# A state-space chunk's decay with the larger of two sums instead of a minimum with zero, its exponential head by head, and one multiply of the norm on GpSimd

## The chip, the cores and the metric

The kernel runs on one core of one Trainium2 chip. Its time is the device time of one execution in microseconds (us); the figure given is the median of the runs. The engines are named as in the profile: PE is TensorE's matmul, PEld its weight load, DVE is VectorE, ACT is ScalarE, POOL is GpSimd, SP is SyncE, which here starts transfers.

## The reference, cut to what matters

One inference step of a two-layer trunk for a prompt of 512 rows and a sample of 64 rows, 1024 columns wide. A layer projects the normed rows, sends part of the columns through a state-space scan (32 heads of 64 in 4 groups, state 128), part through windowed attention, merges both and adds a feed-forward block. The change lies in the scan and in the norm behind it:

```python
def step(state, inp):                      # one chunk, all heads
    xdt, da, bc, cc = inp
    acum = jnp.cumsum(da, axis=1)          # da = dt * a, a < 0: the sums fall
    seg = acum[:, :, None, :] - acum[:, None, :, :]
    decay = jnp.exp(jnp.where(causal[None, :, :, None], seg, -jnp.inf))
    cb = jnp.einsum("blgn,bsgn->blsg", cc, bc)
    y_in = jnp.einsum("blsg,blsgh,bsghp->blghp", cb, decay, xg)
    y_past = jnp.einsum("blgn,bghpn->blghp", cc, sg) * jnp.exp(acum)...
    tail = jnp.exp(acum[:, -1:] - acum)...
    new = sg * jnp.exp(acum[:, -1])... + jnp.einsum("blgn,blgh,blghp->bghpn", bc, tail, xg)
    return new, y_in + y_past
...
y = (y + xh * d_skip[:, None]).reshape(b, L, D_INNER) * jax.nn.silu(z)
y = rmsnorm(y.reshape(b, L, SSM_GROUPS, D_INNER // SSM_GROUPS), ssm_norm_g)   # x / rms, times a weight
```

## The kernel before, in words

All 576 rows (512 of the prompt, 64 of the sample) go through the layer together; activations stand with the columns on the 128 partitions and the rows along the free side. A large product is computed three times over, so that it comes out near full precision: `dps += hh*whi`, `dps += hh*wlo`, `dps += hl*whi` (L278, L279, L280), one 128x288 matmul each. `whi` is the rounded weight tile, made on ACT (L166), and `wlo` what the rounding left, made from `raw` and `whi` by POOL or DVE (L167). Weight tiles of the kinds `whi` and `wlo` have four buffers each.

The state-space part of a group g is a generator, `ssd(g)`, whose steps are let in between the units of the large products of the same stretch: one step of it behind each unit. There are five chunks in each of the 4 groups of the 2 layers, so 40 chunks: 32 of 128 rows and 8 of 64. A chunk goes through

- `step_a`: PE turns the chunk's `xT` (`xn`, L860) and multiplies B and C (`cb`, L862); `bc` holds the cumulative sums of the group's 8 heads along the free side, on every partition (loaded from `ac_dr`, a copy in DRAM). `seg` is the decay of the chunk, 8 heads x 128 x 128: DVE subtracts the sums of the partition's own row (L156, `seg<-bc,ac`), takes the minimum with zero (L869, `seg<-seg`), and ACT does one exponential over all of it (L159, `seg<-seg`). ACT then raises `bc` itself, for the part that comes from the state before.
- `step_p`: DVE makes `xd`, `xw` (input times step and times tail), then `seg<-seg,cbm` and `bc<-bc,BC`.
- `step_s`: `bn`, `xwh`, `xwl`, the pieces of B and of `xw` for the new state.
- `step_b`: PE multiplies `yp` (16 small matmuls, L916 `yp<-seg,xd` and, from the second chunk on, L921 `yp<-bc,S`) and `sp` (L926); DVE adds `yp` into `xT` (L153) and updates the state `S`.

`norm_g(g)` divides the group's gated output by its root mean square: `gbc` holds 1/rms on every partition (ACT copies it out of PSUM, L1035 and L1038). For four blocks of 128x576, DVE multiplies by it (L156, `xT<-xT,gbc`), ACT scales and rounds into `yh` (L159) and DVE makes the rest `yl` (L153). `yh` and `yl` are the moving operands of the group's branch product, which comes later.

Each engine works through its instructions in the order of the program. A scheduler sets that order when the kernel is built, so one edit can move instructions that the edit doesn't touch, on every engine.

## Time and profile before

| | |
|---|---|
| median of 3 runs | 2574.25 us (2573.8 to 2574.63) |
| profiled execution: its own time | 2575.55 us |
| profiled execution: its span | 2573.8 us |
| busy share of the span: PE, DVE, ACT, POOL | 98%, 63%, 41%, 41% |
| instructions: PE, DVE, ACT, POOL | 19609, 2991, 2383, 968 |

The span is the time from the first to the last recorded instruction; the profiled execution took 1.75 us more than that, and 1.30 us more than the median of the runs. A time such as 1411.94 is counted from the start of the span. PE is busy nearly all the time, so the kernel can change its time only through the 2% in which PE stands idle, through the clock at which PE runs, or by taking PE's work late.

### The profile page before, as it was taken

What the parts mean: (1) busy time and instruction counts of PE and PEld (TensorE: products, weight loads), DVE (VectorE), ACT (ScalarE), POOL (GpSimd) and SP (SyncE); (2) the same over time, 40 slices, a digit from 0 to 9 for tenths busy, and PEclk for the clock granted to TensorE, in tenths of its full rate; (3) what the DMA queues carried; (4) which work ended last, traced back from release to release, by engine and by line L of the source; (5) the groups of instructions that cost most, each with busy time, mean ns of one, the idle gap of its engine ahead of it and who ended that gap; (6) DMA issues with size and microseconds to landing.
All of it is one profiled execution on the core that took longest, in us unless ns stands there. A gap on an engine that the chain in (4) does not pass through costs nothing.

```text
span 2573.8 us, 49262 instructions
## 1 busy us (share of the span) xinstructions
PE 2520.1 (98%) x19609; PEld 2395.0 (93%) x19609; DVE 1611.3 (63%) x2991; ACT 1060.8 (41%) x2383; POOL 1054.9 (41%) x968
## 2 busy tenths in 40 slices
PE   7999999999999999999999999999999999999999
PEld 6888999999889999999988899999988999999999
DVE  4598677745765765565686995956467656444443
ACT  3445454443453532222355454543444445323222
POOL 3444455343225754444586464553422266000000
PEclk8999999999999999999999999999999999999999
DMA  8555523243224555545574333332321255222222
GB/s 230 159 157 157 152 86 99 81 103 76 54 58 118 162 166 155 166 140 154 158 183 128 91 95 103 93 102 79 94 70 50 78 147 150 83 83 83 83 79 75
DMA packets 464107, 294.34 MB, mean 114 GB/s; under 512 B 69093, under 2 KB 446405, under 8 KB 463877
## 3 DMA queue, kind: packets, MB, share of 16 engines
q1 hardware_dynamic: 463876, 291.18, 39.4%
q8 instruction: 155, 2.54, 0.4%
q14 instruction: 76, 0.61, 0.1%
HBM read 276.98 MB, written 13.16 MB: 113 GB/s over the span
## 4 chain that ended last, share of the span: by engine, by line
PE 74%; DVE 14%; issue 3%; POOL 2%; ACT 1%; DMA 1%; ACTq 0%; SPq 0%; POOLq 0%; DVEq 0%
PE dps L278 22%; PE dps L280 22%; PE dps L279 21%; DVE cv L153 3%; DVE xT L153 2%; DVE seg L156 1%; PE sc L1213 1%; POOL wlo L167 1%; PE pv L1276 1%; PE pT L1260 1%; PE sp L926 1%; DVE hl L156 1%; PE yp L916 1%; DVE bc L156 1%; DVE S L156 1%
## 5 line engine op out<-in xcount | busy, mean ns | idle before, releaser
L167 POOL TENSOR_TENSOR wlo<-raw,whi 128x512 fp32r<-128x512 f32 (+1 forms) x632 | 896.8, 1427 | 857.6 <-ACT whi L166 743.7
L278 PE MATMUL dps<-hh,whi 128*128 128x288 f32 x3536 | 1055.8, 299 | 4.0 <-ACT hh L672 2.8
L279 PE MATMUL dps<-hh,wlo 128*128 128x288 f32 x3536 | 1050.0, 297 | 2.4 <-POOL wlo L167 2.4
L280 PE MATMUL dps<-hl,whi 128*128 128x288 f32 x3536 | 1049.7, 297 | 1.2 <-DVE hl L156 1.1
L166 ACT CAST whi<-raw 128x512 fp32r<-128x512 f32 (+1 forms) x762 | 462.0, 610 | 555.6 <-PE dps L280 433.2
L278 PEld LDWEIGHTS dps<-hh,whi 128*128 128x128 f32 x3536 | 665.1, 188 | 26.1 <-issue 16.4
L279 PEld LDWEIGHTS dps<-hh,wlo 128*128 128x128 f32 x3536 | 666.3, 188 | 11.3 <-issue 5.4
L280 PEld LDWEIGHTS dps<-hl,whi 128*128 128x128 f32 x3536 | 665.9, 188 | 8.1 <-issue 5.3
L279 PE MATMUL dps<-ah,wlo 128*128 128x288 f32 x704 | 210.8, 299 | 3.7 <-POOL wlo L167 3.7
L278 PE MATMUL dps<-ah,whi 128*128 128x288 f32 x704 | 207.8, 296 | 3.1 <-ACT ah L166 2.6
L280 PE MATMUL dps<-al,whi 128*128 128x288 f32 x704 | 208.3, 296 | 0.0
L153 DVE SCALAR_TENSOR_TENSOR ada_acc<-araw,csl,ada_acc 128x1024 f32<-128x1024 f32 x98 | 153.2, 1602 | 70.1 <-DMA araw<-in_ada_w_dram 66.2
L153 DVE SCALAR_TENSOR_TENSOR cv<-u,colB,cv 128x579 f32<-128x579 f32 x144 | 146.1, 1014 | 30.3 <-ACT cv L159 22.9
L278 PE MATMUL dps<-yh,whi 128*128 128x288 f32 x512 | 153.0, 299 | 1.2 <-ACT u L808 1.1
L280 PE MATMUL dps<-yl,whi 128*128 128x288 f32 x512 | 153.8, 300 | 0.0
L279 PE MATMUL dps<-yh,wlo 128*128 128x288 f32 x512 | 151.7, 296 | 0.0
L279 PEld LDWEIGHTS dps<-ah,wlo 128*128 128x128 f32 x704 | 132.8, 189 | 6.7 <-POOL wlo L167 5.5
L167 DVE TENSOR_TENSOR wlo<-raw,whi 128x512 fp32r<-128x512 f32 (+1 forms) x124 | 83.7, 675 | 87.2 <-ACT whi L166 85.8
L278 PEld LDWEIGHTS dps<-ah,whi 128*128 128x128 f32 x704 | 132.6, 189 | 4.0 <-ACT ah L166 2.8
L280 PEld LDWEIGHTS dps<-al,whi 128*128 128x128 f32 x704 | 132.8, 189 | 0.2 <-DVE al L167 0.2
L278 PEld LDWEIGHTS dps<-yh,whi 128*128 128x128 f32 x512 | 97.3, 190 | 4.5 <-issue 1.9
L280 PEld LDWEIGHTS dps<-yl,whi 128*128 128x128 f32 x512 | 97.3, 190 | 2.0 <-issue 1.8
(326 smaller groups left out, 3863.6 us busy)
## 6 DMA issues: line engine op xcount, KB each, us to landing
raw<-in_w_in_dram SPq DMA_DIRECT2D x119, 512.0 KB
raw<-in_w_gate_up_dram SPq DMA_DIRECT2D x100, 512.0 KB
araw<-in_ada_w_dram SPq DMA_DIRECT2D x56, 512.0 KB
bc<-ac_dr SPq DMA_DIRECT2D x32, 512.0 KB
raw<-in_w_br_ssm_dram SPq DMA_DIRECT2D x32, 512.0 KB
raw<-in_w_out_dram SPq DMA_DIRECT2D x32, 512.0 KB
raw<-in_w_down_dram SPq DMA_DIRECT2D x32, 512.0 KB
raw<-in_ada_w_dram SPq DMA_DIRECT2D x24, 512.0 KB
```

The source lines that it names most:

```text
L153: V.scalar_tensor_tensor(out=out, in0=in0, scalar=scalar, in1=in1, op0=op0, op1=op1)
L156: V.tensor_tensor(out=out, in0=in0, in1=in1, op=op)
L166: S.copy(out=hi, in_=src)
L167: (eng or V).tensor_tensor(out=lo, in0=src, in1=f32(hi), op=ALU.subtract)
L278: T.matmul(ps, lhsT=wh, rhs=rh, start=a == 0, stop=False)
L279: T.matmul(ps, lhsT=wl, rhs=rh, start=False, stop=False)
L280: T.matmul(ps, lhsT=wh, rhs=rl, start=False, stop=a == nk - 1)
L916: T.matmul(yp[64 * r:64 * r + 64, m * 128:m * 128 + Lc], lhsT=xd[0:Lc, h, :], rhs=seg[0:Lc, h, 0:Lc], start=m == 0, stop=sprev is None and ...
L926: T.matmul(sp, lhsT=bn[0:Lc, i], rhs=xw[j], start=a == 0, stop=a == 2)
L1213: T.matmul(ps[:, pi * 192:pi * 192 + nk], lhsT=q[64 * r:64 * r + 64, pi, ch].rearrange("p h q -> p (h q)"), rhs=kT[64 * r:64 * r + 64, t, ...
L1260: T.transpose(ps[0:n, pi * 128:(pi + 1) * 128], s[:, r, pi, 64 * pi * (half is not None):][:, 0:n], ident)
L1276: T.matmul(ps[64 * r:64 * r + 64, 0:256], lhsT=vn[0:n, vt, cols[r]], rhs=pts[r][0:n, 0:256], start=True, stop=half is None)
```

## The change

`ac`, the cumulative sums with the row on the partition, becomes `nac`, the same with the sign turned, and so does the copy in DRAM from which `bc` is loaded. The decay of a chunk was exp(min(bc - ac, 0)). Now DVE takes the larger of the negated sums, max(bc, nac), and ACT computes exp(-seg + nac) head by head: eight instructions of 128x128 with a bias for each partition in place of one of 128x1024. The minimum with zero on DVE is gone. In `norm_g` the multiply by `gbc` runs on POOL and not on DVE.

```diff
-            ac = sm("ac", [128, 5, 32], bufs=1)
-            V.tensor_copy(out=ac.rearrange("p c h -> p (c h)"), in_=ps[:, 0:160])
+            nac = sm("nac", [128, 5, 32], bufs=1)
+            V.tensor_scalar(out=nac.rearrange("p c h -> p (c h)"), in0=ps[:, 0:160], scalar1=-1.0, scalar2=None,
+                            op0=ALU.mult)
...
-            tt(tw.rearrange("p c h -> p (c h)"), ps[:, 160:320], ac.rearrange("p c h -> p (c h)"), ALU.subtract)
+            tt(tw.rearrange("p c h -> p (c h)"), ps[:, 160:320], nac.rearrange("p c h -> p (c h)"), ALU.add)
...
-            S.copy(out=aT[:, 0:512], in_=p1[0:32, :])
-            S.copy(out=aT[:, 512:576], in_=p2[0:32, 0:64])
+            S.mul(out=aT[:, 0:512], in_=p1[0:32, :], mul=-1.0)
+            S.mul(out=aT[:, 512:576], in_=p2[0:32, 0:64], mul=-1.0)
...
                 tt(sg, bc[0:Lc, :, 0:Lc],
-                   st["ac"][0:Lc, ch, h0:h0 + 8].unsqueeze(2).to_broadcast([Lc, 8, Lc]), ALU.subtract)
-                V.tensor_scalar(out=sg, in0=sg, scalar1=0.0, scalar2=None, op0=ALU.min)
-                act(seg[0:Lc, :, 0:Lc], seg[0:Lc, :, 0:Lc], ACTF.Exp)
+                   st["nac"][0:Lc, ch, h0:h0 + 8].unsqueeze(2).to_broadcast([Lc, 8, Lc]), ALU.max)
+                for h in range(8):
+                    act(seg[0:Lc, h, 0:Lc], seg[0:Lc, h, 0:Lc], ACTF.Exp, scale=-1.0,
+                        bias=st["nac"][0:Lc, ch, h0 + h:h0 + h + 1])
                 if ch != 0:
-                    act(bc[:, :, 0:Lc], bc[:, :, 0:Lc], ACTF.Exp)
+                    act(bc[:, :, 0:Lc], bc[:, :, 0:Lc], ACTF.Exp, scale=-1.0)
...
             for j in range(4):
-                tt(y[:, j], y[:, j], bcs, ALU.mult)
+                G.tensor_tensor(out=y[:, j], in0=y[:, j], in1=bcs, op=ALU.mult)
```

The scheduler answers by moving other instructions. On PE, at the head of group 0 of layer 1, the program before has the turn of the first chunks' `xT` (`xn`) and the large product (`dps`) in this order:

```order
L956 MATMUL si<-ident,sld 128x128 x4
L860 MATMUL xn<-ident,xT 64x128 x3
L862 MATMUL cb<-BC 64x64
L864 MATMUL cb<-ident,BC 64x128
L278 MATMUL dps<-hh,whi 128x288
...
L279 MATMUL dps<-hh,wlo 128x288
L860 MATMUL xn<-ident,xT 64x128
L280 MATMUL dps<-hl,whi 128x288
...
L280 MATMUL dps<-hl,whi 128x288
L860 MATMUL xn<-ident,xT 128x128 x4
L862 MATMUL cb<-BC 128x128
```

and the changed program has there:

```order
L959 MATMUL si<-ident,sld 128x128 x4
L861 MATMUL xn<-ident,xT 64x128 x2
L863 MATMUL cb<-BC 64x64
L861 MATMUL xn<-ident,xT 64x128
L865 MATMUL cb<-ident,BC 64x128
L278 MATMUL dps<-hh,whi 128x288
...
L280 MATMUL dps<-hl,whi 128x288
L861 MATMUL xn<-ident,xT 128x128 x3
L863 MATMUL cb<-BC 128x128
...
L278 MATMUL dps<-hh,whi 128x288
L861 MATMUL xn<-ident,xT 128x128
L279 MATMUL dps<-hh,wlo 128x288
L861 MATMUL xn<-ident,xT 64x128
```

The last 64x128 turn of `xT` stood behind 17 `dps` matmuls, counted from the `cb` rows; it now stands behind 35. The lines 860 to 865 are the same as 859 to 864 of before, moved by one.

On POOL, at the norm of the fourth group of layer 0 (`ss` sums squares, `g_y` is the power that makes 1/rms), the program before has:

```order
L1018 TENSOR_TENSOR ss<-ss,nt 128x288 x2
L167 TENSOR_TENSOR wlo<-raw,whi 128x512 x2
L1018 TENSOR_TENSOR ss<-ss,nt 128x288
L167 TENSOR_TENSOR wlo<-raw,whi 128x512
L149 TENSOR_TENSOR g_y<-gv,mhalf 128x5
L167 TENSOR_TENSOR wlo<-raw,whi 128x512 x81
L149 TENSOR_TENSOR n_y<-nv,mhalf 128x3
```

and the changed program:

```order
L1021 TENSOR_TENSOR ss<-ss,nt 128x288
L167 TENSOR_TENSOR wlo<-raw,whi 128x512
L149 TENSOR_TENSOR g_y<-gv,mhalf 128x5
L167 TENSOR_TENSOR wlo<-raw,whi 128x512
L1045 TENSOR_TENSOR xT<-xT,gbc 128x576 x4
L167 TENSOR_TENSOR wlo<-raw,whi 128x512 x80
L149 TENSOR_TENSOR n_y<-nv,mhalf 128x3
```

The four multiplies now stand in one piece between two tiles of `wlo`; 80 tiles follow them, where 81 in a row stood before.

On DVE, at the last chunk of group 3 of layer 0 (`acc` takes the results of the branch product), the program before has:

```order
L156 TENSOR_TENSOR xd<-xn,dtv 128x512
L156 TENSOR_TENSOR xw<-xn,tw 128x512
L156 TENSOR_TENSOR seg<-bc,ac 128x1024
L156 TENSOR_TENSOR cbm<-cb,triu 128x128
L156 TENSOR_TENSOR acc<-acc,dps 128x288 x2
L869 TENSOR_SCALAR seg<-seg 128x1024
L156 TENSOR_TENSOR acc<-acc,dps 128x288
L156 TENSOR_TENSOR bc<-bc,BC 128x1024
L156 TENSOR_TENSOR seg<-seg,cbm 128x1024
L153 SCALAR_TENSOR_TENSOR xT<-xT,dsk_292,yp 128x128 x4
L156 TENSOR_TENSOR S<-S,el 128x512
```

and the changed program:

```order
L156 TENSOR_TENSOR xd<-xn,dtv 128x512
L156 TENSOR_TENSOR xw<-xn,tw 128x512
L156 TENSOR_TENSOR seg<-bc,nac 128x1024
L156 TENSOR_TENSOR cbm<-cb,triu 128x128
L156 TENSOR_TENSOR acc<-acc,dps 128x288 x3
L156 TENSOR_TENSOR seg<-seg,cbm 128x1024
L153 SCALAR_TENSOR_TENSOR xT<-xT,dsk_292,yp 128x128 x4
L156 TENSOR_TENSOR S<-S,el 128x512
L156 TENSOR_TENSOR bc<-bc,BC 128x1024
```

L869 is gone, and `bc<-bc,BC` has moved from ahead of `seg<-seg,cbm` to behind the four additions to `xT` and the step of the state. On ACT, at the same chunk, the program before has:

```order
L166 CAST xwh<-xw 128x512
L166 CAST bn<-cb 128x128
L166 CAST whi<-raw 128x512 x2
L159 ACTIVATE bc<-bc 128x1024
L159 ACTIVATE seg<-seg 128x1024
L166 CAST xwh<-xw 128x512
L166 CAST bn<-cb 128x128
```

and the changed program:

```order
L166 CAST xwh<-xw 128x512
L166 CAST bn<-cb 128x128
L166 CAST whi<-raw 128x512 x2
L159 ACTIVATE seg<-seg,nac 128x128 x8
L159 ACTIVATE bc<-bc 128x1024
L166 CAST xwh<-xw 128x512
L166 CAST bn<-cb 128x128
```

The eight exponentials of `seg` now come ahead of that of `bc`.

## Rows read from the trace of the kernel before

**Rows 1.** The page, part 1: busy us by engine, share of the span, instructions.

```profile
PE 2520.1 (98%) x19609; PEld 2395.0 (93%) x19609; DVE 1611.3 (63%) x2991; ACT 1060.8 (41%) x2383; POOL 1054.9 (41%) x968
```

**Rows 2.** Busy time by engine in the two state-space stretches, granted clock, DMA.

```profile
110.00:520.00 410.00, 402.00 (x3321) 374.18 (x3320) 313.49 (x526) 191.84 (x380) 193.27 (x180) 1.00 0.43 127
1385.00:1800.00 415.00, 404.45 (x3281) 388.90 (x3280) 321.47 (x536) 200.85 (x397) 210.15 (x188) 0.99 0.33 95
```

**Rows 3.** PE's waits: 110 to 520 us (first two), 1385 to 1800 us (total, times, longest).

```profile
PE si L956 <- DMA sld<-in_state_ssm_dram: 2.4, 1, 2.4
PE sp L926 <- DVE xT L153: 1.9, 1, 1.9
...
PE sp L926 <- DVE xT L153: 3.9, 2, 2.0
PE xn L860 <- DVE xT L153: 2.4, 1, 2.4
```

**Rows 4.** Timeline of PE around 1412 us: start, duration, instruction, idle time before it.

```profile
1411.81 0.29 PE L278 MATMUL dps<-hh,whi 128*128 128x288 f32 x1
1411.94 0.29 PE L279 MATMUL dps<-hh,wlo 128*128 128x288 f32 x1
1414.67 0.30 PE L860 MATMUL xn<-ident,xT 128*64 128x128 f32 x1 [2.44 <-DVE xT L153]
1414.73 0.38 PE L280 MATMUL dps<-hl,whi 128*128 128x288 f32 x1
...
1415.45 0.45 PE L278 MATMUL dps<-hh,whi 128*128 128x288 f32 x1
1415.69 0.45 PE L279 MATMUL dps<-hh,wlo 128*128 128x288 f32 x1
```

**Rows 5.** Busy times and PE's granted clock, 1415 to 1418.5 us.

```profile
1415.00:1418.50 3.50, 3.50 (x18) 3.49 (x18) 3.50 (x5) 1.42 (x3) 0.91 (x1) 0.53 0.35 96
```

**Rows 6.** Groups by line and shape: busy us, mean ns; idle before and releaser.

```profile
L167 POOL TENSOR_TENSOR wlo<-raw,whi 128x512 fp32r<-128x512 f32 x600 | 856.2, 1435 | 851.7 <-ACT whi L166 738.2 <-issue 38.3 <-PE pT L1263 23.8
...
L159 ACT ACTIVATE seg<-seg 128x1024 f32<-128x1024 f32 x32 | 33.9, 1061 | 22.8 <-DVE seg L869 22.4
...
L156 DVE TENSOR_TENSOR xT<-xT,gbc 128x576 f32<-128x576 f32 x32 | 29.9, 994 | 11.5 <-ACT gbc L1038 11.5
...
L869 DVE TENSOR_SCALAR seg<-seg 128x1024 f32<-128x1024 f32 x32 | 25.9, 810 | 0.0
...
L159 ACT ACTIVATE s<-s,nm 128x128 f32<-128x128 f32 x16 | 6.2, 390 | 10.7 <-DVE nm L153 10.7
```

**Rows 7.** Timeline around the last chunk of group 3, layer 0.

```profile
498.53 1.05 ACT L159 ACTIVATE bc<-bc 128x1024 f32<-128x1024 f32 x1
...
499.77 1.06 ACT L159 ACTIVATE seg<-seg 128x1024 f32<-128x1024 f32 x1 [0.19 <-DVE seg L869]
...
501.89 1.21 DVE L156 TENSOR_TENSOR seg<-seg,cbm 128x1024 f32<-128x1024 f32 x1
...
504.71 1.09 PE L916 MATMUL yp<-seg,xd 128*64 128x128 f32 x16
```

**Rows 8.** Timeline around the norm of group 3, layer 0.

```profile
565.13 0.59 ACT L1035 COPY gbc<-gbp 128x512 f32<-128x512 f32 x1 [0.20 <-PE gbp L1034]
...
565.61 0.22 ACT L1038 COPY gbc<-gbp 128x64 f32<-128x64 f32 x1
...
567.04 1.40 POOL L167 TENSOR_TENSOR wlo<-raw,whi 128x512 fp32r<-128x512 f32 x1 [3.39 <-ACT whi L166]
...
574.19 0.29 PE L279 MATMUL dps<-hh,wlo 128*128 128x288 f32 x1
```

**Rows 9.** Timeline of POOL and DVE at the norm of group 0, layer 0.

```profile
245.07 5.39 POOL L167 TENSOR_TENSOR wlo<-raw,whi 128x512 fp32r<-128x512 f32 x1 [5.45 <-ACT gbc L1038]
...
246.56 2.76 DVE L156 TENSOR_TENSOR xT<-xT,gbc 128x576 f32<-128x576 f32 x4
...
251.26 1.29 POOL L167 TENSOR_TENSOR wlo<-raw,whi 128x512 fp32r<-128x512 f32 x1
```

More of the change, by code (lines that the diff above doesn't have):

```diff
@@ L790, in dt_side @@
             SY.dma_start(out=ac_dr[l][4, :, 0:64], in_=aT[:, 512:576])
-            st.update(dt=dt, ac=ac, el=el, tw=tw)
+            st.update(dt=dt, nac=nac, el=el, tw=tw)
             yield
```

## Prediction, made before the changed kernel ran

> **What bounds the kernel now.** I read the page first. Its line of busy times shows PE at 2520.1 of 2573.8 us, 98%, and DVE, ACT and POOL at 63%, 41% and 41% [rows 1]. So the time is PE's work plus what PE loses, and an edit on DVE, ACT or POOL counts only where PE waits for that engine. The view by windows says how much can be lost or won where the changed instructions stand: in the two state-space stretches PE is busy 402.00 of 410 us and 404.45 of 415 us, so it stands idle for 8.00 + 10.55 = 18.55 us [rows 2]. DVE is busy 313 and 321 us there, ACT 192 and 201, POOL 193 and 210; none of them is near full over the stretch, and what matters is single places.
>
> The view of PE's waits names these places. The longest single waits are one of 2.4 us for the loaded state (`si`), one of 2.4 for DVE's `xT` (`xn`), and three of about 1.9 each, 5.8 in total, of `sp` for DVE's additions to `xT` [rows 3]. The timeline shows one of them with what follows it. Up to 1411.94 the `dps` matmuls start every 0.13 us. Then PE stands for 2.44 us in front of the fourth 64x128 `xn`, and a little later the matmuls start every 0.24 us (1415.45, 1415.69) [rows 4]. The granted clock over 1415.0 to 1418.5 is 0.53 [rows 5]: the lower of the two levels, 1.2 in place of 2.4 GHz, for most of these 3.5 us. The gap thus costs twice: 2.44 us of standing, and about (1 - 0.53) x 3.5 = 1.65 us of slow running behind it.
>
> **The change part by part.**
>
> *The minimum is removed.* DVE loses 32 instructions of 810 ns, 25.9 us busy [rows 6], and 8 short ones, which at half the elements on half the partitions I take at no more than the same 0.81 each, so 6.5 at the most. The larger-of-two that replaces the subtraction has the same operands and shape, so I cost it at no difference. What DVE wins does not reach PE by itself; it has to be looked for at the waits below.
>
> *One exponential becomes eight, on ACT.* The one takes 1061 ns for 128x1024. The nearest row for a 128x128 piece with a bias for each partition is the attention's `s<-s,nm`, 390 ns [rows 6]. Neighbours on ACT overlap: the copy of `gbc` that starts at 565.13 lasts to 565.72, and the next starts at 565.61, 0.11 us earlier [rows 8]. So eight take 8 x (0.39 - 0.11) + 0.11 = 2.35 us, 1.29 more than one. Below, I bound it by no loss (eight as quick as one), above by no overlap at all: 3.12 us, 2.06 more. Over 40 chunks that is 52 us (0 to 82) on an engine that is 41% busy [rows 1]. Is it on the path? At the chunk that I found to be among the tightest, the last of its group, ACT did the exponential of `bc` at 498.53 and that of `seg` from 499.77 to 500.83, because it waited for the minimum on DVE. DVE multiplied by `cbm` from 501.89 to 503.10, and PE used the result at 504.71 [rows 7]: 1.61 us to spare. In the changed order the eight come first, with no minimum to wait for: from 498.53 to 500.88, against 500.83 before. By the upper bound they end at 501.65, which is still before 501.89, where DVE took `seg` up. So the extra work on ACT is hidden by the minimum that is gone and by the exchange with `bc`; the exponential of `bc` ends about 1.1 us later, and DVE's `bc<-bc,BC` stands after the additions to `xT` in the new order anyway. I take 0. If that cover were gone (eight at 3.12 behind a late start), the loss is 2.06 - 1.61 = 0.45 us in each of 8 groups, +3.6 us, my upper bound. Copies with a factor of -1 in place of plain copies (`nac`, `aT`) have the same shapes and stand once in a layer: 0.
>
> *The multiply by 1/rms moves to POOL.* DVE loses 32 of 994 ns, 29.9 us. On POOL the nearest row is `wlo`, two inputs too, 128x512 in 1435 ns; by elements 1435 x 576/512 = 1.61 us each, 52 us in eight bursts of four [rows 6]. The undisturbed one of 1.29 gives 1.45 [rows 9], the lower bound. Queued behind a burst are weight tiles that PE needs. In the fourth group of layer 0 `gbc` is ready at 565.83; POOL then starts `wlo` at 567.04, and it ends at 568.44; I followed that tile by its buffer number to the matmul that first reads it, at 574.19 [rows 8]. That is a reserve of 5.75 us. Now the burst goes first: 565.83 + 4 x 1.61 = 572.27, then 1.40, so 573.67, and 0.52 us are left. I take 0, but the cover is thin: from 574.19 - 1.40 - 565.83 = 6.96, a multiply above 1.74 us makes PE wait. `yh` and `yl` come later by about 4 x (1.61 - 0.99) = 2.5 us; the product that reads them comes behind the one that reads this tile, so that is hidden. The one row that shows what may go wrong is the `wlo` at 245.07, which lasted 5.39 us, 4.10 more than its undisturbed neighbour, while DVE did the multiplies by `gbc` of this norm, two inputs each [rows 9]; by it one multiply alone would lose 4.6 us. I put that at the upper end, among the rivals.
>
> The Trainium skill speaks against this move: its GPSIMD Engine Reference, 4.1 Engine selection, gives elementwise work to VectorE and puts two-input operations on GpSimd at about twice the time. By this rule the price would be an estimated 2 x 0.994 = 1.99 us, the burst would end at 573.79, the tile at 575.19, and PE would wait 1.0 us at each of the two fourth groups, +2.0 on the sum; by the rows (1.61) it waits for nothing. The trace agrees with the direction (1.61 against 0.994 is 1.6 times), not with the full factor.
>
> *What the scheduler moved.* At the head of group 0 of layer 1 the fourth 64x128 `xn` stands behind 35 `dps` matmuls where it stood behind 17. At 0.13 us each [rows 4] PE comes to it 18 x 0.13 = 2.34 us later, with work done meanwhile, so of the 2.44 us wait 0.10 is left: -2.34 (0 if DVE is later by as much, -2.44 at best). With the gap the slow running behind it should go: -1.65 (0 to -1.65). On the other side, PE's order as a whole leaves the run of `dps` matmuls at 394 places, not 382. The first `dps` behind the `xn` lasts 0.38 against 0.29 [rows 4], so 0.09 each: 12 x 0.09 = +1.1 (0 to +2.2, for two turns each).
>
> *The other waits.* `sp` stands at the same places of PE's order. The DVE work in front of it loses a minimum of 0.81, but new neighbours are set before it: 0, between -2.4 and +2.4 (three times 0.81). The wait for the state's load [rows 3] depends on a transfer whose issue and whose use both move: 0, between -2.4 and +1.0.
>
> **The sum.** -2.34 - 1.65 + 1.1 = -2.9 us against the profiled execution's own 2575.55, which gives 2572.65. That execution is 1.30 above the median of the runs, so on the median's scale it is 2574.25 - 2.9 = 2571.35, 2571 us. A measurement of this kernel can tell about 0.2%, 5.1 us, from no change, so this is a change that would not be told.
>
> **The rivals.**
>
> (a) *DVE's relief reaches PE.* DVE loses 56 us or more. For it: DVE is the engine named in four of these five long waits [rows 3]. Against it: these waits end on additions to `xT` that themselves need PE's `yp`, and none names the minimum. If the three `sp` waits go (-5.8), and a slow stretch as in [rows 5] behind two of them (-3.3), the time is 2571.35 - 9.1 = 2562. Chance 0.22.
>
> (b) *POOL's bursts make PE wait* (slower). Place: the `wlo` behind the four multiplies in each norm. Price: at 2.2 us a multiply, halfway from 1.45 to twice that, the tile is ready at 565.83 + 8.8 + 1.40 = 576.03, 1.84 late. At two norms that is +3.7, at all eight +14.7, with the slow running behind half of them +6.6 more: 2575 to 2593, most likely near 2583. It decides from 1.74 us a multiply. For it: the 5.39 us row. Against it: the four operations that DVE ran beside it, from 246.56 on [rows 9], are the very ones that leave DVE. The Trainium skill has the mechanism (GPSIMD Engine Reference, 8 Key points): GpSimd shares its interfaces to SBUF with VectorE and contends with operations with two SBUF inputs. By that rule the 5.39 us row is no accident, which is part of this chance: 0.24, of which 0.18 beyond +0.2%.
>
> (c) *The gap at 1412 only moves.* If DVE's `xT` comes later too, neither -2.34 nor -1.65 is won: 2575.4, no change that can be told. Chance 0.15.
>
> (d) *The eight exponentials come late at the tight chunks.* At 3.12 us and a late start PE's `yp` waits 0.45 to 2 us in each group, some with slow running behind: 2575 to 2587. For it: an engine in order also delays the weight tiles behind. Against: the working above. Chance 0.07, of which 0.05 beyond +0.2%.
>
> **How the numbers follow.** The forecast itself, 2567 to 2575, has 0.32; about 0.10 of it lies below 2569.1, where faster begins. Faster: 0.22 + 0.10 = 0.32. Slower: 0.18 + 0.05 = 0.23. The rest, 0.22 + 0.06 + 0.15 + 0.02 = 0.45, is no change. The range reaches down to (a) at 2562 and up to the likely case of (b) at 2583; beyond them I leave 0.06 below and 0.10 above.
>
> **What would show it.** Right: no wait of 2.4 us of `xn` in the second stretch, no clock of 0.53 behind 1412; ACT busier by some 50 us, POOL by some 50, DVE less by some 55 to 60; the 128x128 exponentials near 0.3 to 0.4 us; multiplies on POOL near 1.6. Wrong: waits of `dps` (L279) for POOL's `wlo` behind each norm; multiplies above 1.74 us; waits of `yp` for `seg`; or PE's idle time in the stretches well under 18.55 us, which would be (a).

## The result, and the profile after

The changed kernel takes 2587.65 us (median of 4 runs, 2587.09 to 2588.38), the kernel before 2574.44 beside it: a ratio of 1.0052, with a 95% interval of 1.0039 to 1.0064. It is slower by 13 us, where 2571 was forecast; the time lies above the stated range. Three single runs that lie far off the others of their kernel (11947 us of the kernel before, 5559 of e2, 3201 of e13) are left out of the medians and ratios below.

The page of the changed kernel, part 1, that answers to [rows 1]:

```profile
PE 2522.5 (98%) x19609; PEld 2394.5 (93%) x19609; DVE 1574.6 (61%) x2919; ACT 1111.9 (43%) x2663; POOL 1089.5 (42%) x1000
```

DVE is 36.7 us less busy (1574.6 against 1611.3), ACT 51 us more, POOL 35 us more. The minimum (25.9) and the multiply (29.9) took 55.8 us of DVE before [rows 6], so at least 19 us of what was taken from DVE came back in other instructions. The windows of the two state-space stretches, that answer to [rows 2]:

```profile
110.00:520.00 410.00, 400.71 (x3297) 371.60 (x3296) 296.96 (x495) 216.57 (x518) 200.34 (x191) 1.00 0.43 126
...
1385.00:1800.00 415.00, 397.86 (x3216) 380.56 (x3217) 310.24 (x498) 223.73 (x534) 217.61 (x197) 0.99 0.32 93
```

PE stands idle for 410 - 400.71 = 9.3 us in the first and for 415 - 397.86 = 17.1 us in the second, 26.4 in place of 18.55, and it gets less done in the same time (3297 and 3216 matmuls, where the kernel before had 3321 and 3281). PE's waits in the second stretch, 1385 to 1800 us, that answer to the second half of [rows 3] (total, times, longest):

```profile
PE sp L929 <- DVE xT L153: 5.4, 2, 2.7
...
PE xn L861 <- DVE xT L153: 2.6, 3, 1.4
...
PE cb L863 <- DVE xT L153: 2.3, 4, 0.8
...
PE sp L929 <- DVE bn L167: 1.7, 1, 1.7
...
PE dps L279 <- POOL wlo L167: 1.6, 2, 0.8
```

Three things are to be seen. The two `sp` waits have grown from 3.9 to 5.4 us. The one wait of `xn` of 2.4 us is now three, 2.6 in total. And of the nine rows of this view seven name DVE and one POOL: what PE mostly waits for is not the weight tile behind POOL's multiplies. The timeline of PE where the gap of 2.44 us stood [rows 4]:

```profile
1415.41 0.30 PE L861 MATMUL xn<-ident,xT 128*64 128x128 f32 x1 [0.89 <-DVE xT L153]
...
1422.40 0.33 PE L861 MATMUL xn<-ident,xT 128*128 128x128 f32 x1 [1.43 <-DVE xT L153]
```

The 64x128 `xn` did move out of its gap, but two turns of `xT` in the neighbourhood now wait 0.89 and 1.43 us, 2.32 together. The clock dip behind it is gone: the granted clock over 1415.0 to 1418.5 is 1.00 here. The groups by line and shape, that answer to [rows 6]:

```profile
L159 ACT ACTIVATE seg<-seg,nac 128x128 f32<-128x128 f32 x256 | 79.6, 390 | 35.1 <-DVE seg L156 35.0
...
L1045 POOL TENSOR_TENSOR xT<-xT,gbc 128x576 f32<-128x576 f32 x32 | 55.0, 1749 | 16.8 <-ACT gbc L1041 16.8
...
L156 DVE TENSOR_TENSOR seg<-bc,nac 128x1024 f32<-128x1024 f32 x32 | 50.8, 1588 | 11.2 <-PE yp L919 9.3 <-DMA bc<-ac_dr 2.0
...
L156 DVE TENSOR_TENSOR seg<-seg,cbm 128x1024 f32<-128x1024 f32 x32 | 47.6, 1487 | 3.3 <-ACT seg L159 2.6
...
L153 DVE SCALAR_TENSOR_TENSOR yl<-xT,colA,yh 128x576 fp32r<-128x576 f32 x32 | 38.9, 1225 | 25.2 <-ACT yh L159 25.2
```

The exponentials cost what was forecast (390 ns each). A multiply on POOL takes 1749 ns, just above the 1740 from which PE was expected to wait. What the prediction had not costed stands in the next rows. The larger of two, `seg<-bc,nac`, takes 1588 ns where the subtraction took 1450 in the kernel before:

```profile
L156 DVE TENSOR_TENSOR seg<-bc,ac 128x1024 f32<-128x1024 f32 x32 | 46.4, 1450 | 9.6 <-PE yp L916 9.2 <-DMA bc<-ac_dr 0.4
```

`seg<-seg,cbm` takes 1487 (1254 before). And in front of `yl` DVE stood idle for 25.2 us, waiting for ACT's `yh`; before, it stood idle at that point of the norm too, 11.5 us in front of the multiply by `gbc` [rows 6]. At the norm of the fourth group, that answers to [rows 8]:

```profile
568.99 0.22 ACT L1041 COPY gbc<-gbp 128x64 f32<-128x64 f32 x1
...
569.28 6.64 POOL L1045 TENSOR_TENSOR xT<-xT,gbc 128x576 f32<-128x576 f32 x4 [2.26 <-ACT gbc L1041]
...
575.89 1.81 POOL L167 TENSOR_TENSOR wlo<-raw,whi 128x512 fp32r<-128x512 f32 x1
...
571.55 1.16 DVE L153 SCALAR_TENSOR_TENSOR yl<-xT,colA,yh 128x576 fp32r<-128x576 f32 x1 [8.06 <-ACT yh L159]
```

DVE has nothing to do here for 8.06 us. Most of this is not POOL's doing: `gbc` itself was ready only at 569.21, and 2.34 us are left for the first multiply and `yh`. PE lost only 0.8 us around this place (from 558 to 598), as the next table shows. It gives the start of the n-th `dps` matmul in each run's profiled execution, as a difference from the kernel before (us); a column that jumps shows where time is lost:

```
    n   before   changed   decay half   POOL half   decay half + 4 idle multiplies
  338    112.1      +0.4         +2.0        +1.4        +0.3
 1756    375.7      -0.6         -2.8        +2.5        -0.5
 2124    437.0      +3.4         -4.5        +6.5        +4.1
 2847    557.9      +3.4         -4.4        +6.5        +4.1
 3120    597.9      +4.2         -4.4        +7.3        +4.9
 8283   1383.7      +5.2         -3.9        +8.4        +6.5
 9059   1524.9      +8.4         -3.8        +9.8        +8.1
 9257   1564.9     +10.5         -7.2       +10.5        +6.8
 9653   1625.1     +10.6         -7.1       +10.6        +6.9
 9985   1685.5     +13.6        -10.0       +13.7       +10.2
15903   2568.3     +11.8        -11.1       +13.6        +9.5
```

The changed kernel loses 4.0 us from 376 to 437 and 8.4 from 1384 to 1686, right behind the norms of the first groups, where the convolution and the chunks of the next group run, and little elsewhere.

### The profile page after: what moved, and what is told of

It is laid out like the page before. It is cut to its first block, busy times and chain, and to the rows that moved or that the text cites. A ratio compares the mean times of both kernels' runs of the same rounds, so it can differ in the third digit from the quotient of the medians.

```text
span 2585.6 us, 49504 instructions
## 1 busy us (share of the span) xinstructions
PE 2522.5 (98%) x19609; PEld 2394.5 (93%) x19609; DVE 1574.6 (61%) x2919; ACT 1111.9 (43%) x2663; POOL 1089.5 (42%) x1000
## 4 chain that ended last, share of the span: by engine, by line
PE 44%; DVE 8%; ACT 2%; issue 2%; DMA 1%; POOL 1%; ACTq 0%; DVEq 0%; POOLq 0%; SPq 0%
PE dps L278 13%; PE dps L280 13%; PE dps L279 13%; DVE cv L153 2%; DVE ada_acc L153 1%; POOL wlo L167 1%; DVE seg L156 1%; DMA araw<-in_ada_w_dram 1%; PE sc L1216 1%; DVE xT L153 1%; ACT cv L159 1%; PE pv L1279 0%; ACT seg L159 0%; PE sp L929 0%; PE pT L1263 0%
## 5 line engine op out<-in xcount | busy, mean ns | idle before, releaser
L167 POOL TENSOR_TENSOR wlo<-raw,whi 128x512 fp32r<-128x512 f32 (+1 forms) x632 | 884.5, 1409 | 823.3 <-ACT whi L166 717.9
L278 PEld LDWEIGHTS dps<-hh,whi 128*128 128x128 f32 x3536 | 663.8, 188 | 26.4 <-issue 17.0
L159 ACT ACTIVATE seg<-seg,nac 128x128 f32<-128x128 f32 (+1 forms) x320 | 95.8, 379 | 46.8 <-DVE seg L156 46.7
L166 ACT CAST ah<-gate 128x288 fp32r<-128x288 f32 x88 | 37.8, 431 | 151.8 <-DVE gate L156 151.5
```

What stands on the lines that cost most here:

```text
L159: S.activation(out=out, in_=in_, func=func, **kw)
L166: S.copy(out=hi, in_=src)
L167: (eng or V).tensor_tensor(out=lo, in0=src, in1=f32(hi), op=ALU.subtract)
L278: T.matmul(ps, lhsT=wh, rhs=rh, start=a == 0, stop=False)
```

## The experiments

All lines of DVE, ACT and POOL not named are as in the kernel on which the experiment is built; the scheduler places anew each time. Ratios are to the kernel before, run beside it. The single runs of one kernel lie up to 12 us apart (e4: 2565 to 2578), so that two medians 3 us apart are not told from each other.

**The two halves.** e1 keeps the multiply on DVE:

```diff
-                G.tensor_tensor(out=y[:, j], in0=y[:, j], in1=bcs, op=ALU.mult)
+                tt(y[:, j], y[:, j], bcs, ALU.mult)
```

> The decay half of the change alone: negated sums, larger of two, eight exponentials; the multiply by 1/rms stays on DVE. Theory A (in the changed kernel DVE, working in order, stands before seg<-seg,cbm and bc<-bc,BC until ACT has done eight exponentials of 390 ns and then that of bc, and the convolution and the inputs of the next chunk queue behind it): most of the loss stays, 2581 to 2587 us, with PE's idle time in the second state-space stretch near 15 us or more. Theory B (the loss comes from the four multiplies in a row on POOL at 1.75 us each, which delay the weight tiles and yh): 2571 to 2576. Theory C (the two halves cost about the same, or the scheduler's placing decides, whatever is edited): 2577 to 2581.

Measured: 2564.48 us (median of 8 runs), ratio 0.9965 (0.9953 to 0.9976): faster by 9 us, below all the expectations. e2 is the kernel before with the same line turned the other way:

> The other half alone: the kernel before with the multiply by 1/rms on POOL. Theory A: only the two norms of the fourth groups make PE wait for wlo, about 1 us each, so 2574 to 2578 us. Theory B: nearly the whole loss, 2583 to 2588, with PE waiting for wlo behind most norms. Theory C: 2578 to 2582.

Measured: 2589.14 us (median of three), ratio 1.0053 (1.0036 to 1.0070). So theory B names the right half: the decay part gains about 10 us, the multiply on POOL loses about 14 on the kernel before and, in the changed kernel, 23 on e1. But the reason that B gave is not borne out: in e2 too, PE waits for `wlo` only 0.5 us in the second stretch. Windows of e1 in the two stretches:

```profile
110.00:520.00 410.00, 407.28 (x3364) 379.20 (x3363) 301.37 (x514) 217.78 (x522) 180.42 (x182) 1.00 0.44 129
...
1385.00:1800.00 415.00, 406.13 (x3334) 389.97 (x3334) 307.88 (x521) 225.84 (x538) 199.86 (x189) 1.00 0.34 97
```

PE's idle time is 2.7 + 8.9 = 11.6 us, against 18.55 before and 26.4 with both halves. The clock adds to it. In e1 the granted clock is 1.00 all through both stretches. In the changed kernel it falls four times, to 0.57 in the 4 us from 405 and from 1565.5 and to 0.62 in the 4.5 us from 1497 and from 1681.5, three of them right behind a stop of PE of 2.7 us for `sp`. PE runs at the lower level, 1.2 GHz, for most of that time; (1 - 0.57) x 4 = 1.7 us are lost each time, 6.8 in all. The 14.8 us more of standing and these 6.8 of slow running make up 21.6 of the 23 us between e1 and the changed kernel.

**What gains in the decay half.** e3 is e1 with one exponential without bias, so its decay is not the reference's:

```diff
-                for h in range(8):
-                    act(seg[0:Lc, h, 0:Lc], seg[0:Lc, h, 0:Lc], ACTF.Exp, scale=-1.0,
-                        bias=st["nac"][0:Lc, ch, h0 + h:h0 + h + 1])
+                act(seg[0:Lc, :, 0:Lc], seg[0:Lc, :, 0:Lc], ACTF.Exp, scale=-1.0)
```

> The decay half, multiply by 1/rms on DVE, but with one exponential of 128x1024 (scale -1, no bias) in place of the eight: the bias is left out, so the decay computed is not that of the reference. DVE has no minimum, ACT has no extra work. Theory A: the loss is gone and DVE's relief is left, 2568 to 2575 us. Theory B: the same as e1, 2571 to 2576. Theory C: anywhere from 2570 to 2582, and not ordered by ACT's work.

Measured: 2563.39 us, ratio 0.9956 (0.9938 to 0.9973), 1 us from e1. e4 takes the kernel before, and only splits its exponential into eight:

```diff
-                act(seg[0:Lc, :, 0:Lc], seg[0:Lc, :, 0:Lc], ACTF.Exp)
+                for h in range(8):
+                    act(seg[0:Lc, h, 0:Lc], seg[0:Lc, h, 0:Lc], ACTF.Exp)
```

> The kernel before, with its subtraction and minimum on DVE and its multiply by 1/rms on DVE; only the one exponential is split into eight of 128x128 without a bias. Theory A: ACT's extra 2 us a chunk now comes behind the minimum as well, so slower than before by 8 us or more: 2582 to 2592. Theory B: no part of the loss, 2574 to 2577. Theory C: 2574 to 2582.

Measured: 2573.05 us, ratio 0.9992 (0.9979 to 1.0005): no difference. Its row (mean of one 128x128 without a bias):

```profile
L159 ACT ACTIVATE seg<-seg 128x128 f32<-128x128 f32 x256 | 55.2, 298 | 23.2 <-DVE seg L869 22.8
```

Theory A falls with both: the eight exponentials cost PE nothing that can be told, on either decay. What is left to gain is that the minimum is gone from DVE, and the new order that came with it; no run takes the minimum away and keeps the order, so their shares are not told apart. Why a relief of DVE reaches PE is seen in two windows of 60 us of the kernel before, which the prediction did not look at, and the same windows of e1 below them (us; busy time of PE, PEld, DVE, ACT, POOL):

```profile
355.00:415.00 60.00, 58.04 (x485) 55.41 (x484) 59.20 (x92) 29.42 (x57) 31.37 (x29) 1.00 0.32 95
...
1620.00:1680.00 60.00, 58.11 (x477) 55.63 (x476) 58.62 (x91) 29.30 (x57) 30.41 (x30) 0.97 0.30 89
```

```profile
355.00:415.00 60.00, 59.72 (x496) 57.13 (x496) 56.87 (x90) 36.31 (x88) 28.47 (x29) 1.00 0.33 100
...
1620.00:1680.00 60.00, 59.70 (x496) 57.11 (x495) 56.39 (x92) 36.26 (x88) 28.46 (x28) 1.00 0.35 105
```

Before, DVE is busy 59.20 and 58.62 of 60 us. Over the 410 and 415 us of [rows 2] it was 76 and 77%; here it is nearly full, and PE stands 2 us in each window. In e1 DVE is busy 56.87 and 56.39 us, and PE stands 0.3. e5 exchanges the exponentials of `bc` and `seg` in e1:

```diff
+                if ch != 0:
+                    act(bc[:, :, 0:Lc], bc[:, :, 0:Lc], ACTF.Exp, scale=-1.0)
                 for h in range(8):
                     act(...)
-                if ch != 0:
-                    act(bc[:, :, 0:Lc], bc[:, :, 0:Lc], ACTF.Exp, scale=-1.0)
```

> The decay half (e1) with the exponential of bc ahead of the eight of seg in the code of step_a. DVE stood idle 9.4 us in front of bc<-bc,BC in e1, waiting for ACT. If the order of these two matters to PE: 2558 to 2562 us when seg is not late, 2566 to 2572 when it is. If ACT's work is off the path, as e3 and e4 say: 2562 to 2566, the same as e1.

Measured: 2565.98 us, ratio 0.9970 (0.9957 to 0.9984): the same as e1, so ACT's order there does not matter either.

**Why the POOL half loses: waiting, or POOL's work beside DVE.** Three kernels on e1. e6 adds work on POOL whose results nothing reads:

```diff
+            sh = sm("gsh", [128, 128], bufs=1)
             for j in range(4):
+                for i in range(3):
+                    b = bcs[:, i * 128:(i + 1) * 128]
+                    G.tensor_tensor(out=sh, in0=b, in1=b, op=ALU.mult)
                 tt(y[:, j], y[:, j], bcs, ALU.mult)
```

> The decay half (e1), multiplies by 1/rms on DVE as they are, and besides them twelve multiplies of 128x128 on POOL in each norm, gbc by gbc into a tile that nobody reads: about 7 us of POOL's time with two inputs each, on which yh and yl do not wait. Theory W (the loss of the POOL half is the wait: yh on ACT and yl on DVE stand in their queues until POOL has multiplied, and what is behind them is late): 2562 to 2568 us, near e1's 2564.5. Theory N (the loss is POOL's time beside DVE: operations of DVE with two inputs get longer while POOL works, and weight tiles and the small copies on POOL come later): most of the 23 us between e1 and the changed kernel, so 2576 to 2590, with DVE's seg<-bc,nac above 1.4 us in the mean where e1 has 1.25.

Measured: 2571.14 us, ratio 0.9987 (0.9975 to 0.9999), 6.7 us above e1: between the two theories, with `seg<-bc,nac` up to 1398 ns (in a profiled execution that took 2579.55 us, the longest of its ten).

```profile
L1048 POOL TENSOR_TENSOR gsh<-gbc 128x128 f32<-128x128 f32 x96 | 70.3, 732 | 15.8 <-ACT gbc L1038 10.5
...
L156 DVE TENSOR_TENSOR seg<-bc,nac 128x1024 f32<-128x1024 f32 x32 | 44.7, 1398 | 9.6 <-PE yp L919 9.3 <-DMA bc<-ac_dr 0.3
```

e8 puts only the last of the four multiplies on POOL:

```diff
-                tt(y[:, j], y[:, j], bcs, ALU.mult)
+                if j == 3:
+                    G.tensor_tensor(out=y[:, j], in0=y[:, j], in1=bcs, op=ALU.mult)
+                else:
+                    tt(y[:, j], y[:, j], bcs, ALU.mult)
```

> The decay half (e1), with only the last of the four multiplies of each norm on POOL. POOL's part (1.4 to 1.9 us) runs beside DVE's first three (0.67 each), so that yh waits for nearly nothing. Theory W: 2560 to 2566 us. Theory N: a quarter of the loss, 2568 to 2572.

Measured: 2580.14 us, ratio 1.0026 (1.0016 to 1.0035): 15.7 us above e1, more than either theory gave. The three multiplies that stayed on DVE, with POOL's beside them:

```profile
L156 DVE TENSOR_TENSOR xT<-xT,gbc 128x576 f32<-128x576 f32 x24 | 29.5, 1282 | 13.9 <-ACT gbc L1041 13.9
```

They take 1282 ns, where e1 has 884 (below). The scheduler's order differs more from e1's here than in e6, so a part may be that; the table of sums below says more. e9 leaves POOL a sliver of each multiply, so that `yh` still waits for POOL:

```diff
-                tt(y[:, j], y[:, j], bcs, ALU.mult)
+                tt(y[:, j, 0:544], y[:, j, 0:544], bcs[:, 0:544], ALU.mult)
+                G.tensor_tensor(out=y[:, j, 544:576], in0=y[:, j, 544:576], in1=bcs[:, 544:576], op=ALU.mult)
```

> The decay half (e1), with 544 of the 576 columns of each multiply on DVE and the last 32 on POOL: yh waits for POOL and its queue, but POOL works only some 0.2 to 0.3 us on each. Theory W: a good part of the loss, 2572 to 2585 us. Theory N: little of it, 2564 to 2570.

Measured: 2567.29 us, ratio 0.9973 (0.9964 to 0.9983), 2.8 us above e1, which is not told from it. POOL's slivers took 646 ns each, more than was reckoned. But DVE stood idle 0.0 us in front of `yl` here, against 25.2 in the changed kernel, so e9 tests a much shorter wait than theory W needs and does not price it.

**How POOL's work costs.** e10 doubles e6's multiplies (`for i in (0, 1, 2, 0, 1, 2)`):

> As the run with twelve idle multiplies on POOL in each norm (e6), but with twenty-four. If POOL's time with two inputs is what costs: twice e6's loss against e1, so 2576 to 2583. If e6's 6.7 us was chance of placing: 2566 to 2573.

Measured: 2602.94 us, ratio 1.0108 (1.0091 to 1.0125), 38 us above e1: far more than twice. Its PE waits, 110 to 1800 us, and one wait of ACT ahead of them show another route:

```profile
PE dps L278 <- ACT u L809: 17.7, 3, 6.4
...
PE dps L279 <- POOL wlo L167: 7.6, 8, 2.2
...
391.63 0.69 ACT L159 ACTIVATE ct<-cv 128x579 f32<-128x579 f32 x1 [7.88 <-POOL gsh L1048]
```

PE now waits 17.7 us for ACT to empty `dps` (`u`), and 7.6 for `wlo`. Some 12 us ahead of each of these three long waits, ACT stood 7.9 to 8.3 us in front of the convolution's `ct` until POOL's last idle multiply was done. `ct`, `cv` and `gbc` share two buffers in the program (the tag `wt`), so work that reads `gbc` for longer holds a buffer that `ct` needs. So e10 can't be read as a double dose of the same, and nor is e6 free of it: there ACT stood 2.45 us in front of `ct` at three norms. e11 takes fills in place of multiplies, which read nothing:

```diff
-                for i in range(3):
-                    b = bcs[:, i * 128:(i + 1) * 128]
-                    G.tensor_tensor(out=sh, in0=b, in1=b, op=ALU.mult)
+                if j == 0:
+                    G.tensor_copy(out=sh[:, 0:1], in_=bcs[:, 0:1])
+                for i in range(7):
+                    G.memset(sh, 0.0)
```

> As e6, but POOL's idle work reads nothing: 28 fills of 128x128 in each norm, some 6 to 8 us, in place of twelve multiplies; PE's order is the same as with these but for four rows. If DVE's operations with two inputs are held up only by a POOL that reads (the 128x1024 rows of seg at 1.25 us as in e1): 2563 to 2567. If it is the queue on POOL (weight tiles and small copies late by the same 7 us): 2569 to 2575, as e6.

Measured: 2564.48 us, ratio 0.9962 (0.9947 to 0.9977): the time of e1, with 46 us more on POOL. (That the hundredths agree is luck.)

```profile
L1049 POOL MEMSET gsh<- 128x128 f32 x224 | 45.8, 205 | 11.6
...
L156 DVE TENSOR_TENSOR seg<-bc,nac 128x1024 f32<-128x1024 f32 x32 | 41.1, 1284 | 9.5 <-PE yp L919 9.3 <-DMA bc<-ac_dr 0.2
```

e13 doubles the fills (`range(14)`):

> As the run with 28 idle fills on POOL in each norm (e11), with 56: 11.5 us a norm at the 0.205 us that a fill took, 92 us in all, more than the 70 us of the twelve multiplies (e6) and less than the 120 of the twenty-four (e10). If only a POOL that reads costs: 2563 to 2568, as e11. If POOL's time as such costs: 2573 to 2590, between e6 and e10.

Measured: 2571.55 us, ratio 0.9992 (0.9981 to 1.0004), about 7 us above e1; of the 7.3 us by which its profiled execution stands behind e1's, 3.3 are there at 112 us, ahead of the first norm. So fills for 11.5 us a norm may cost something too, and this run leaves open whether it is 0 or 7. The cleanest run is e12: POOL's work in the form of the changed kernel, behind DVE's multiplies, with results that nothing reads:

```diff
+            for j in range(4):
+                G.tensor_tensor(out=bcs, in0=bcs, in1=bcs, op=ALU.mult)
             st.pop(("y", g))
```

> The decay half (e1), multiplies by 1/rms on DVE, and behind them in each norm four idle multiplies of 128x576 on POOL, gbc by gbc into itself, on which neither yh nor yl waits: POOL's work of the changed kernel in size and form, without its wait; eight rows of PE's order and none of DVE's differ from e1. If the held-up operations of two inputs are the main part of the loss: 2571 to 2583, with POOL's multiplies at 1.6 to 1.9 us. If the wait of yh and yl is the main part: 2564 to 2568.

Measured: 2583.58 us, ratio 1.0038 (1.0025 to 1.0052), 19 us above e1 and slower than before, with the orders of DVE and of ACT the same as e1's. Its groups, and the longest wait of PE in its first stretch, with the same instruction in e1 behind it:

```profile
L1050 POOL TENSOR_TENSOR gbc<-gbc 128x576 f32<-128x576 f32 x32 | 52.1, 1628 | 13.2 <-DVE xT L156 12.4
...
L156 DVE TENSOR_TENSOR seg<-bc,nac 128x1024 f32<-128x1024 f32 x32 | 45.2, 1414 | 12.5 <-PE yp L919 9.3 <-DMA bc<-ac_dr 3.1
...
L153 DVE SCALAR_TENSOR_TENSOR yl<-xT,colA,yh 128x576 fp32r<-128x576 f32 x32 | 50.0, 1593 | 0.0
...
389.59 0.77 PE L863 MATMUL cb<-BC 128*128 128x128 f32 x2 [4.00 <-DVE xT L153]
```

```profile
383.56 0.46 PE L863 MATMUL cb<-BC 128*128 128x128 f32 x2 [0.26 <-DVE xT L153]
```

`yl`, which DVE does while POOL multiplies, takes 1593 ns where e1 has 1219, and `seg<-bc,nac` 1414. PE then stands 4.00 us for DVE's additions of `yp` to `xT`, which are queued behind them. At this place the account closes. From the norm's first multiply by `gbc` to these additions DVE runs the same 32 instructions in both kernels and stands idle for the same 1.94 us. Against the quickest tenth of their kind they lose 7.07 us in e12 and 3.32 in e1, so 3.75 more, and PE's wait is 3.74 longer. Of the 3.75, 2.75 were lost beside the idle multiplies and 1.00 beside tiles of `wlo`. Layer 1 repeats it at the same place: 7.06 us against 3.33, and a wait of 3.99 us against 0.28. With the slow running behind them these two places lose 6.5 and 6.3 us against e1. Not all of e12 is as clean: at one norm, from 1536.7 to 1540.25, ACT stood for the buffer of `gbc`, as in e10; there e12 lost 1.2 us against e1. So most of the loss comes without any wait for the result of the multiply.

A sum over all of DVE shows beside which instruction of POOL the time goes: for each DVE instruction, what its duration has above that of the quickest tenth of its kind and shape (in the kernel before, e1 and the changed kernel), where that is over 0.1 us, put to the POOL instruction that overlaps it longest, and added up over 110 to 520 and 1385 to 1800 us of each profiled execution. The last column is the time of that execution.

```
run                            DVE longer, us   beside wlo   beside multiplies   time, us
decay half (e1)                     72.2           68.3             -             2564.4
28 idle fills (e11)                 72.0           68.0             -             2562.8
56 idle fills (e13)                 74.7           71.0             -             2571.8
sliver on POOL (e9)                 73.6           70.7            0.0            2564.6
12 idle small multiplies (e6)       80.7           69.7            7.2            2579.6
last multiply on POOL (e8)          92.2           83.3            6.0            2579.3
4 idle multiplies (e12)             95.2           76.0           15.9            2585.0
changed kernel                      92.5           73.5           16.0            2587.3
kernel before                       82.9           81.0             -             2575.6
POOL half (e2)                      96.6           79.0           16.0            2589.1
```

The four multiplies of a norm hold DVE up by 16 us wherever they stand on POOL. But most of what DVE loses, in every run, is lost beside `wlo`, and this part moves by up to 15 us with the order alone: in e8 it is 83.3 against e1's 68.3, so there most of the loss is not beside the one multiply that moved.

## Why the prediction was wrong, point by point

**Removing the minimum: wrong, by about -10 us.** The prediction said that DVE's gain does not reach PE by itself and gave this rival 0.22. e1 and e3 show that it does: 2564.5 and 2563.4, near the 2562 of rival (a). The step that failed is the reading of [rows 2]: "none of them is near full over the stretch". A share over 400 us hid stretches of 60 us in which DVE is busy 98%. How much of the 10 us is the minimum itself stays open: DVE also lost 10.7 us less beside POOL in e1 than before (72.2 against 82.9), all of it beside `wlo` (68.3 against 81.0), which the change of order can have brought.

**Eight exponentials: right.** 390 ns each and 2.45 us for a burst of eight (forecast 2.35), 51 us more on ACT (forecast 52), and nothing on PE's path that can be told (e3, e4, e5).

**The multiply on POOL: the step that decided, wrong by about +23 us.** Its price was near (1.75 us against 1.61). What failed is "I take 0", whose only cover was the reserve of the weight tile. That tile was hardly waited for (1.6 us in the second stretch). Rival (b) had the side and, in its contention, the mechanism, but looked for it on POOL: the multiplies get longer and `wlo` is late. That its range, 2575 to 2593, holds the measured time is therefore luck in part. It is DVE that loses. The two-input operations of DVE that run beside POOL's get longer, and PE waits for what stands behind them in DVE's queue. At the norm of the second group of layer 0 the changed kernel has this burst of multiplies and, beside its last one, an operation of DVE:

```profile
362.81 7.13 POOL L1045 TENSOR_TENSOR xT<-xT,gbc 128x576 f32<-128x576 f32 x4
...
368.85 2.18 DVE L156 TENSOR_TENSOR seg<-bc,nac 128x1024 f32<-128x1024 f32 x1
```

The same happens beside a tile of `wlo`. In e1, at the chunk behind the norm of the second group of layer 0, DVE has (start, duration):

```profile
385.53 1.21 DVE L156 TENSOR_TENSOR seg<-bc,nac 128x1024 f32<-128x1024 f32 x1
...
389.39 1.21 DVE L156 TENSOR_TENSOR seg<-seg,cbm 128x1024 f32<-128x1024 f32 x1
...
385.62 2.28 POOL L167 TENSOR_TENSOR wlo<-raw,whi 128x512 fp32r<-128x512 f32 x1
```

and the changed kernel at the same chunk, with POOL's instruction beside each, and the wait of PE that follows:

```profile
387.66 2.36 POOL L167 TENSOR_TENSOR wlo<-raw,whi 128x512 fp32r<-128x512 f32 x1 [1.45 <-ACT whi L166]
...
388.98 2.12 DVE L156 TENSOR_TENSOR seg<-bc,nac 128x1024 f32<-128x1024 f32 x1
...
395.12 1.29 POOL L167 TENSOR_TENSOR wlo<-raw,whi 128x512 fp32r<-128x512 f32 x1 [2.59 <-ACT whi L166]
...
395.19 2.30 DVE L156 TENSOR_TENSOR seg<-seg,cbm 128x1024 f32<-128x1024 f32 x1
...
404.13 0.47 PE L929 MATMUL sp<-xwh,bn 128*128 128x512 f32 x1 [2.70 <-DVE xT L153]
```

2.12 and 2.30 us in place of 1.21 each. In e1 a tile of `wlo` stands beside `seg<-bc,nac` too; but there DVE began 0.09 us earlier and was done in 1.21, and POOL took 2.28. In the changed kernel POOL began first, and DVE paid: at 395.12 POOL began 0.07 us ahead and took 1.29, its undisturbed time, and DVE took 1.09 more than 1.21. All 88 operations of DVE with two inputs of 128x1024 can be sorted this way. Of the 62 in the changed kernel that began with no two-input operation of POOL under way, none took more than 1.23 us, also the 24 beside which POOL began one later; of the 26 that began with one under way, 24 took longer, 2.29 us in the median (of the other two, one began 0.09 us ahead of POOL's end, and the other beside a `wlo` of 3.17 us, which was held up itself). In e1 only 10 began so, and 4 took longer. The Trainium skill (SBUF — State Buffer, section SBUF: two separate sides) has it that whichever of the two starts first holds the shared ports for the whole instruction; these counts agree. So not only POOL's time counts, but whether its instructions begin ahead of DVE's. Beside the multiplies stand only 4 of those 24, beside `wlo` 20: the growth of these rows is for the most part a shift of `wlo` against DVE that came with the new order, while of the 16 us beside the multiplies 9.4 fall on `cv`, 2.4 on `yl` and 4.1 on these rows. In e1 the rows of both operations, of the multiply that stays on DVE, and of `yl` are:

```profile
L156 DVE TENSOR_TENSOR seg<-bc,nac 128x1024 f32<-128x1024 f32 x32 | 40.1, 1254 | 10.1 <-PE yp L919 9.3 <-DMA bc<-ac_dr 0.7
...
L156 DVE TENSOR_TENSOR seg<-seg,cbm 128x1024 f32<-128x1024 f32 x32 | 40.4, 1261 | 3.1 <-ACT seg L159 2.4
...
L156 DVE TENSOR_TENSOR xT<-xT,gbc 128x576 f32<-128x576 f32 x32 | 26.4, 884 | 13.9 <-ACT gbc L1041 13.9
...
L153 DVE SCALAR_TENSOR_TENSOR yl<-xT,colA,yh 128x576 fp32r<-128x576 f32 x32 | 38.0, 1219 | 0.0
```

so the two groups alone grow by 32 x (1588 - 1254 + 1487 - 1261) = 17.9 us in the changed kernel, against 26.4 that the multiply took on DVE in e1. In e2 it is the convolution that pays, 1114 ns a piece where the kernel before (last row) has 1014, 14 us in all:

```profile
L1042 POOL TENSOR_TENSOR xT<-xT,gbc 128x576 f32<-128x576 f32 x32 | 55.1, 1753 | 4.5 <-ACT gbc L1038 4.5
...
L153 DVE SCALAR_TENSOR_TENSOR cv<-u,colB,cv 128x579 f32<-128x579 f32 x144 | 160.5, 1114 | 34.5 <-ACT cv L159 24.0 <-ACT u L812 6.0 <-POOL wlo L167 3.1
...
L153 DVE SCALAR_TENSOR_TENSOR cv<-u,colB,cv 128x579 f32<-128x579 f32 x144 | 146.1, 1014 | 30.3 <-ACT cv L159 22.9 <-ACT u L812 6.0
```

The prediction's argument against (b), that the operations that held up POOL are the ones that leave DVE, was wrong: others of two inputs took their place. The Trainium skill (GPSIMD Engine Reference, 8 Key points) states that GpSimd shares its interfaces with VectorE and contends with operations of two SBUF inputs; e12 agrees (1593 against 1219 for `yl`). Fills, which read nothing, left `seg<-bc,nac` at 1284 in e11, where e1 has 1254.

**The wait of `yh` and `yl`: not named, price open.** "`yh` and `yl` come later by about 2.5 us ... so that is hidden" forgot that `yl` stands in DVE's queue: 25.2 us of idle DVE, where e1 has 13.9 in front of its multiplies by `gbc`, so 11.3 more. All 14 of these waits fall in the norms of the third and fourth groups; around them the table of the n-th `dps` shows no more than 0.8 us lost in layer 0. What the wait of `yh` does in ACT's queue at the other norms, where ACT stood up to 0.86 us for POOL, no run prices.

**The gap at 1412: moved as read, won nothing.** The `xn` moved as read from the order, and the clock dip went. But two other turns of `xT` wait 2.32 us there. By the n-th `dps` the changed kernel gained 1.8 us on the kernel before across the gap (from 1408 to 1415) and had lost 2.5 again by 1436, so nothing of the -4.0 was left. That is rival (c). And it has as many dips of the clock in the two stretches as the kernel before, four, at other places (before: 0.57 in the 4 us from 210, 1415, 1555 and 1667.5).

**The other terms.** The `sp` waits for DVE's `xT`, taken at 0, grew by 2.3 us (from 5.8 to 2.7 + 5.4), within their bounds. The +1.1 for more turns between runs of `dps` was not measured by itself.

**What stays open.** e12 shows 19 of the 23 us without the wait but also without the relief of 26 us on DVE that the changed kernel has. With that relief DVE is less full there: 54.73 and 50.87 of 60 us in the two windows above, and in each it waits 5.1 us for ACT's `cv`, where in e1 it waits 1.4. How the 23 us divide between longer operations, the waits and the new order of PE and DVE was not separated. Nor is it shown what in e8's order puts so much more of DVE's work beside `wlo`.

## What to carry to other kernels

Look for the engine that is full in the 60 us around an edit, not over the stretch: there, work taken from it can reach the time, and so can anything that lengthens its instructions (3.75 us longer on VectorE, 3.74 longer a wait of TensorE). Moving an elementwise operation with two inputs from VectorE to GpSimd was no relief here, where VectorE goes on with such operations; of the two halves of this change the decay half alone is the version to keep, at 2564.5 us (0.9965 of the kernel before). Before calling a moved operation free, look at what its old engine does meanwhile, and not only at what waits behind it on the new one. And an experiment with idle work is only idle if the buffers that it reads are not needed by anybody else.

## What the runs showed of the hardware

A VectorE operation of two inputs in SBUF, 128x1024, takes 1.20 to 1.23 us in the kernel before, in e1 and in the changed kernel whenever no GpSimd operation of two inputs is under way at its start, also when one begins beside it. Begun while one ran, it took up to 2.43 us: 0.07 us behind a GpSimd 128x512 of 1.29 us it took 2.30. Where VectorE began first, it stayed at 1.21 and GpSimd's 128x512 went to 2.28. GpSimd's multiply of 128x576 took 1.41 to 1.44 us in 13 of 32 cases of the changed kernel and 1.93 to 1.96 in 18; one of 128x32 took 0.65 in the mean (e9). Twenty-eight fills of 128x128 a norm on GpSimd, 0.205 us each, left VectorE's sum (72.0 us against 72.2) and the time as they were. ScalarE's 128x128 exponential took 390 ns with a bias tile and 298 without, and a burst of eight with it mostly 2.45 us.
